# A two-layer encoder kernel: other dense blocks in layer 0, and its gathers moved into layer 1's attention stage

## The chip, the cores and the metric

The kernel runs on one core of one Trainium2 chip. The metric is device time in microseconds (us) of one execution, median of three runs. The core has a matrix engine (PE, with its weight loads as PEld), a vector engine (DVE), an activation engine (ACT), GpSimd (POOL) and SyncE (SP); 16 DMA engines move data between device memory and the on-chip memories.

## The reference

512 tokens of width 1024 go through two layers. Each layer has an attention part and an expert part, both with layer normalizations and a conditioning vector around them:

```python
h = _modulate(x, sh1, sc1)
mix = _hybrid_mixer(h, ...)            # MLA | short convolution | stick-breaking, then W_o
x = _layer_norm(DEEPNORM_ALPHA * x + (1 + g1) * mix, ...)
h = _modulate(x, sh2, sc2)
ffn = _peer(h, wq, k1, k2, u_tab, v_tab)
x = _layer_norm(DEEPNORM_ALPHA * x + (1 + g2) * ffn, ...)
```

The attention is causal in blocks of 128 tokens: block b needs the keys of blocks 0 to b. The expert part (PEER) gives every token 8 heads of 16 experts out of 16384: a query, scores against two sets of 128 keys, the top 16 of each, the top 16 of their sums. With the chosen experts' rows u and v (1024 numbers each),

```python
act = gelu(einsum('tkd,td->tk', u[experts], h))
out = einsum('tk,tkd->td', g * act, v[experts])
```

so a token's result sums 128 rows of v.

## The kernel before

**Blocks.** The tokens are four blocks of 128 (0 to 3). In the expert part two blocks of a layer are done *densely* and two by *gathers*; before, the dense ones are 1 and 2 in both layers (`DENSE`, L35).

**Dense blocks** (`dense`). For 256 tokens at once, all 16384 experts are worked through in 128 tiles of 128 experts. A tile's u and v rows (512 KB each) are loaded by SP; u is transposed on PE and split in two parts (ACT L819, DVE L821); three matmuls per slice make the scores (L831 to L833); ACT makes the Gelu, DVE multiplies by G, the gate weights spread out to a matrix over experts; two pairs of matmuls add the products with v (L849). G is made by `build` in three chunks: 32 builds ahead of the loop, 64 more beside the first 85 tiles. At the end each dense block's sum goes through `finish` (residual, layer normalization).

**Gathered blocks** (`experts`). For each of the 128 (head, rank) slots of a block, POOL issues an indirect DMA that fetches one row of u for each of 128 tokens (L696, 512 KB), and DVE multiplies it with h2 and sums (L698); then the same slot's row of v is fetched (L708) and added to the block's sum (L713). The slots go in four groups of 32: 32 u rows, a Gelu, 32 v rows. So a block is 256 gathers and a layer 512. Four buffers `g` (pool `gath`, L62) are shared by all; the block's sum `acc`, `h2`, `dots` and `wts` are single. The last slot is followed by `finish`, which writes the block's new x.

**Pacing** (`pace`). The gathers of a layer are one sequence, block by block. `EARLY[l]` of them are put ahead of the dense part and so run in the layer's own attention stage, as soon as the first gathered block's experts are known. 32 are paired with the 32 first builds, `LATE[l]` are left over for the next layer's attention stage (L956, L903), and the rest is spread evenly over the 128 tiles (L952). Within the paced part the DVE operation of a gather is ordered behind that of its tile. Before: 80 early, 350 in the loop and 50 late in layer 0; 110 early, 370 and 0 in layer 1.

**Attention stage.** Blocks 0 and 1 are normalized (`prepare`) and projected together, then attended one after the other; each goes through W_o (`output`), the normalizations (`between`), the queries (`queries`) and the top 16 (`topk`). Blocks 2 and 3 are prepared after block 1's attention and projected together: in `gemm` each weight tile serves block 2 and then block 3. `behind` puts that projection's first matmul behind the last query matmul of block 0. The top 16 of block 3 waits until the first builds are through (L950). In layer 0 the stage also computes the conditioning of both layers (`ada_side`) on DVE, ACT and POOL.

**Order.** The instruction order of each engine is planned at build time: a scheduler goes through the program with estimated times, and where several are ready takes the one that comes earlier in the program; on the chip each engine keeps that order. The late gathers stand ahead of the next layer's attention in the program.

Of the kernel before, what the change touches and what calls it, by code (L numbers as in the profile page):

```python
# [21 lines left out]
P = 128  # L22
# [3 lines left out]
NB = S // P  # L26
# [5 lines left out]
TG = 8  # L32
TI = 4
CUTS = (0, 43, 85, 128)
DENSE = (1, 2)  # L35
EARLY = (80, 110)
LATE = (50, 0)
WK = 4
ADK = 2
HB = 2  # L40
# [13 lines left out]
def body(ctx, tc, x, c, positions, ada_w, ada_b, w_in, q_norm_g, kv_norm_g, w_uq, w_ukv, conv_w,  # L54
         w_o, ln1_g, ln1_b, peer_wq, peer_k1, peer_k2, peer_u, peer_v, ln2_g, ln2_b, out):
    nc = tc.nc
# [89 lines left out]
    h2tok = [dram.tile([2, P, D], F32, name=f"h2tok{l}") for l in range(L)]  # L146
# [74 lines left out]
    def row_op(y, dst, src, i, op, mk=None, scalar=None, op0=None):  # L221
        for g in range(2):
            sl = slice(g * 512, (g + 1) * 512)
            pm = mk() if mk else A.ps.tile([P, 512], F32, name="prow", tag="mm", bufs=2)
            for c0 in range(2):
                r = 4 * i + 2 * g + c0
                nc.tensor.matmul(pm[:, c0 * 256:(c0 + 1) * 256], lhsT=sel[0:96, r:r + 1].to_broadcast([96, P]),
                                 rhs=y.rows[0:96, :], start=True, stop=True)
            if scalar is None:
                last = nc.vector.tensor_tensor(dst[:, sl], src[:, sl], pm, op=op)  # L230
            else:
                last = nc.vector.scalar_tensor_tensor(dst[:, sl], src[:, sl], scalar, pm, op0=op0, op1=op)
        return last
# [21 lines left out]
    def affine(y, dst, tmp, src, ig, ib, mk=None, pool=None):  # L255
        mean, r = moments(src, pool)
        row_op(y, tmp, src, ig, OP.mult, mk, mean, OP.subtract)
        return row_op(y, dst, tmp, ib, OP.add, mk, r, OP.mult)
# [89 lines left out]
    def exp_ln(first):  # L348
        ld = nc.scalar.preload_act_table_set("natural_log_exp_and_others")
        order(ld, first)  # L350
        return ld
# [222 lines left out]
    def between(y, b, rt, mk=None):  # L574
        l = y.l
        row_op(y, rt, rt, 7, OP.mult, mk)
        nc.vector.scalar_tensor_tensor(rt, xs[b], ALPHA, rt, op0=OP.mult, op1=OP.add)
        affine(y, xs[b], rt, rt, 0, 1, mk)
        h2 = A.work.tile([P, D], F32, name="h2d", tag="tok", bufs=2)
        affine(y, h2, h2, xs[b], 2, 3, mk)  # L580
        h2T = A.work.tile([P, KT, P], F32, name="h2T", tag="tok", bufs=2)
        transpose_cols(h2T, h2, KT, tag="tr" if mk else "mm")
        if b in DENSE:
            slot = DENSE.index(b) * P
            nc.sync.dma_start(h2scr[l][:, :, slot:slot + P], h2T)
        else:
            nc.sync.dma_start(h2tok[l][b // 2], h2)
        v1 = topp.tile([P, 2 * PH, TOPK], F32, name="tk_v", bufs=2)
        fi = topp.tile([P, PH, 2, TOPK], F32, name="tk_f", bufs=2)
        return h2T, v1, fi  # L590
# [89 lines left out]
    def experts(y, b, eidx, gw):  # L680
        def after(inst):
            if gate[0] is not None:
                tc.add_manual_dep(inst.ins, gate[0].ins.name,
                                  mybir.DependencyInfo(mybir.DependencyClass.NoSync, mybir.DependencyReason.DATA),
                                  reason="expert sums in pace with the dense tiles")

        h2 = pw.tile([P, D], F32, name="h2")
        nc.sync.dma_start(h2, h2tok[y.l][b // 2])
        acc = pw.tile([P, D], F32, name="acc")
        dots = pw.tile([P, PH, TOPK], F32, name="dots", bufs=1)  # L690
        wts = pw.tile([P, PH, TOPK], F32, name="wts", bufs=1)
        for h0 in range(0, PH, HB):
            slots = [(h, k) for h in range(h0, h0 + HB) for k in range(TOPK)]
            for j, (h, k) in enumerate(slots):
                g = gath.tile([P, D], F32, name="g")
                nc.gpsimd.indirect_dma_start(out=g, out_offset=None, in_=u_flat,  # L696
                                             in_offset=bass.IndirectOffsetOnAxis(ap=eidx[:, h, k:k + 1], axis=0))
                after(nc.vector.scalar_tensor_tensor(out=g, in0=g, scalar=1.0, in1=h2, op0=OP.mult, op1=OP.mult,  # L698
                                                     accum_out=dots[:, h, k:k + 1]))
                yield  # L700
            hs = slice(h0, h0 + HB)
            ge = nc.scalar.activation(wts[:, hs, :], dots[:, hs, :], AF.Gelu)
            if b == 0 and h0 < 2:
                exp_ln(ge)
            nc.vector.tensor_tensor(wts[:, hs, :], wts[:, hs, :], gw[:, hs, :], op=OP.mult)
            for j, (h, k) in enumerate(slots):
                g = gath.tile([P, D], F32, name="g")
                nc.gpsimd.indirect_dma_start(out=g, out_offset=None, in_=v_flat,  # L708
                                             in_offset=bass.IndirectOffsetOnAxis(ap=eidx[:, h, k:k + 1], axis=0))
                if h == 0 and k == 0:  # L710
                    r = nc.vector.tensor_scalar(acc, g, wts[:, h, k:k + 1], None, op0=OP.mult)
                else:
                    r = nc.vector.scalar_tensor_tensor(out=acc, in0=g, scalar=wts[:, h, k:k + 1], in1=acc,  # L713
                                                       op0=OP.mult, op1=OP.add)
                after(r)
                if h < PH - 1 or k < TOPK - 1:
                    yield
        tc.cur_priority -= 1000000
        finish(y, b, acc, lambda: psx.tile([P, 512], F32, name="prow", tag="ex"), pw)
        tc.cur_priority += 1000000  # L720
        yield

    def finish(y, b, acc, mk, pool):
        row_op(y, acc, acc, 4, OP.mult, mk)
        nc.vector.scalar_tensor_tensor(acc, xs[b], ALPHA, acc, op0=OP.mult, op1=OP.add)
        r = affine(y, xs[b], acc, acc, 5, 6, mk, pool)
        if y.l == L - 1:
            nc.sync.dma_start(out[0, b * P:(b + 1) * P, :], xs[b])
        return r
# [164 lines left out]
    def pace(ex, mark, n):  # L894
        gate[0] = mark
        for _ in range(n):
            next(ex)

    ada_first(range(4))
    for l in range(L):  # L900
        if l:
            open_attention(l)
            late()  # L903
        y = layer_setup(l)

        def pick(b, v1, fi):
            return topk(l, v1, fi, b, b not in DENSE)

        res = [None] * NB
        for b in (0, 1):  # L910
            prepare(y, b)
        layer_keys(y)
        ps = project(y, (0, 1))
        if l + 1 < L:
            ada_side(0, range(4, 12))
        layer_rows(y)
        behind = None
        for p in ps:
            b = p[0]
            attend(y, *p)  # L920
            if b == 1:
                for b2 in (2, 3):
                    prepare(y, b2)
            h = between(y, b, output(y, b, p[2]))
            r = queries(y, *h, range(4))
            if b == 0:
                behind = r
            res[b] = pick(b, *h[1:])
        p2, p3 = project(y, (2, 3), behind)
        if l + 1 < L:  # L930
            ada_side(1, range(12))
        attend(y, *p2)
        h = between(y, 2, output(y, 2, p2[2]))
        queries(y, *h, range(2))
        attend(y, *p3)
        rt = output(y, 3, p3[2])
        queries(y, *h, range(2, 4))
        res[2] = pick(2, *h[1:])
        h = between(y, 3, rt, lambda: A.ps.tile([P, 512], F32, name="prow", tag="at", bufs=2))
        queries(y, *h, range(4))  # L940
        res[3] = partial(pick, 3, *h[1:])
        A.stack.close()
        dn = dense(y, DENSE, res)
        ex = chain.from_iterable(experts(y, b, *res[b]) for b in range(NB) if b not in DENSE)
        pace(ex, None, EARLY[l])
        groups = 2 * P // TG
        for _ in range(groups):
            mark = next(dn)
            pace(ex, mark, 1)
        with tc.issue_after(mark.ins):  # L950
            res[3] = res[3]()
        n = 2 * 2 * NSLOT - EARLY[l] - LATE[l] - groups  # L952
        for a, mark in enumerate(dn):
            if a < NK:
                pace(ex, mark, (a + 1) * n // NK - a * n // NK)
        late = partial(pace, ex, mark, LATE[l])  # L956
        if not l + 1 < L:
            late()
# [22 lines left out]
```

## Time and profile before

| | |
|---|---|
| median of 3 runs | 3552.92 us (3548.99 to 3555.07) |
| profiled execution | 3562.45 us, its span 3560.7 us |
| granted clock of PE, mean | 0.921 of full speed |
| PE / DVE / POOL / ACT busy | 88% / 77% / 41% / 26% of the span |
| moved by DMA | 1012 MB, mean 284 GB/s |
| layer 0: attention stage, first build | 0 to 687.2 us |
| layer 0: dense loop's combining matmuls | 783.0 to 1782.9 us |
| layer 1: attention stage, first build | to 2442.7 us |
| layer 1: dense loop's combining matmuls | 2540.3 to 3536.0 us |

The span is the time from the first to the last instruction of the profiled execution. A busy share is an average over stages with different limits, so the table is read by stage. A group's row names the line, the engine, the operation, output and inputs, the count, the busy time and mean duration, and then the engine's idle time just before it with what ended most of it.

### The profile page before, as it was taken

How to read it: one execution, taken by the hardware profiler on the slowest of the kernel's cores; microseconds unless marked ns; L12 is line 12 of the kernel's file. 1: busy time of each engine (PE TensorE's matmuls, PEld its weight loads, DVE VectorE, ACT ScalarE, POOL GpSimd, SP SyncE). 2: the span in 40 equal slices, each digit the busy share in tenths (PEclk: the TensorE clock that was granted, in tenths of full speed). 3: DMA queues.
4: the chain of work that ended last, by engine and by line, in shares of the span. 5: the costliest groups of instructions: out<-in, count | busy, mean ns of one | idle time of the engine just before them, and what ended most of it. 6: DMA issues, size and time to landing. Idle time of an engine off the chain costs nothing.

```text
span 3560.7 us, 54292 instructions
## 1 busy us (share of the span) xinstructions
PE 3131.7 (88%) x19708; PEld 2331.2 (65%) x19708; DVE 2753.5 (77%) x6085; ACT 925.9 (26%) x1860; POOL 1455.3 (41%) x1347
## 2 busy tenths in 40 slices
PE   6889778659999999999948896786799999999998
PEld 3567546547777777777736784565577777777775
DVE  4668996999777867676775589889998787776777
ACT  2342432222222222222122223312222222222221
POOL 1025573255434334444451045533454444444443
PEclk9989879859999999999969996897799999999998
DMA  8778978568888888899985586885789988889997
GB/s 269 221 231 261 312 253 278 178 196 293 314 314 312 307 285 313 314 344 347 337 286 194 177 297 208 288 297 172 256 284 335 333 320 310 319 309 336 360 351 257
DMA packets 430171, 1012.13 MB, mean 284 GB/s; under 512 B 40504, under 2 KB 229192, under 8 KB 429904
## 3 DMA queue, kind: packets, MB, share of 16 engines
q0 software_dynamic: 147456, 536.94, 42.3%
q1 hardware_dynamic: 282448, 471.73, 39.3%
q8 instruction: 156, 2.56, 0.3%
q14 instruction: 111, 0.91, 0.1%
HBM read 1002.06 MB, written 6.34 MB: 283 GB/s over the span
## 4 chain that ended last, share of the span: by engine, by line
PE 18%; DVE 11%; DMA 9%; issue 8%; POOL 3%; ACT 1%; SPq 0%; POOLq 0%; DVEq 0%; ACTq 0%
PE pm L157 5%; DMA g<-in_peer_v,eidx 5%; PE acc L849 5%; DVE acc L713 2%; POOL g L696 2%; DVE g L698 2%; DMA g<-in_peer_u,eidx 2%; DMA wt<-in_peer_wq 1%; PE sp L831 1%; PE sp L832 1%; PE sp L833 1%; PE utp L817 1%; DMA wt<-in_w_in 1%; DVE o L797 1%; DVE tk_ef L668 1%
## 5 line engine op out<-in xcount | busy, mean ns | idle before, releaser
L708 POOL DMA_INDIRECT g<-in_peer_v,eidx x512 | 616.0, 1203 | 806.0 <-DVE acc L713 553.3
L849 PE MATMUL acc<-v,ge 128*128 128x512 f32 x2048 | 926.7, 595 | 0.9 <-DMA v<-in_peer_v 0.5
L696 POOL DMA_INDIRECT g<-in_peer_u,eidx x512 | 582.2, 1137 | 765.6 <-DVE g L698 546.7
L713 DVE SCALAR_TENSOR_TENSOR acc<-g,wts,acc 128x1024 f32<-128x1024 f32 x508 | 673.7, 1326 | 149.6 <-DMA g<-in_peer_v,eidx 146.1
L698 DVE SCALAR_TENSOR_TENSOR g<-g,h 128x1024 f32<-128x1024 f32 x512 | 622.2, 1227 | 152.6 <-DMA g<-in_peer_u,eidx 151.3
L831 PE MATMUL sp<-hh,uh 128*128 128x256 f32 x2048 | 612.9, 299 | 4.2 <-ACT ge L835 4.2
L849 PEld LDWEIGHTS acc<-v,ge 128*128 128x128 f32 x2048 | 371.5, 191 | 367.3 <-issue 366.5
L833 PE MATMUL sp<-hh,ul 128*128 128x256 f32 x2048 | 594.8, 290 | 0.0
L832 PE MATMUL sp<-hl,uh 128*128 128x256 f32 x2048 | 583.4, 285 | 0.0
L819 ACT CAST uh<-utp 128x512 fp32r<-128x512 f32 x512 | 304.7, 596 | 866.5 <-PE utp L817 728.9
L821 DVE TENSOR_TENSOR ul<-utp,uh 128x512 fp32r<-128x512 f32 x512 | 346.4, 683 | 117.0 <-ACT uh L819 116.3
L831 PEld LDWEIGHTS sp<-hh,uh 128*128 128x128 f32 x2048 | 391.3, 191 | 10.2 <-ACT ge L835 5.1
L832 PEld LDWEIGHTS sp<-hl,uh 128*128 128x128 f32 x2048 | 391.5, 191 | 4.8 <-issue 4.8
L833 PEld LDWEIGHTS sp<-hh,ul 128*128 128x128 f32 x2048 | 390.7, 191 | 0.0
L817 PE MATMUL utp<-ident,u 128*128 128x128 f32 x2048 | 304.9, 278 | 25.1 <-DVE ul L821 21.9
L804 PEld LDWEIGHTS <-o 128*128 128x128 bf16 x4608 | 222.0, 117 | 152.2 <-DVE o L797 79.0
L806 ACT COPY G<-pg 128x344 f32<-128x344 f32 (+1 forms) x192 | 147.1, 766 | 618.0 <-PE pg L804 618.0
L804 PE MATMUL pg<-o,o 128*128 128x43 bf16 (+1 forms) x4608 | 235.8, 219 | 80.4 <-DVE o L797 75.7
L817 PEld LDWEIGHTS utp<-ident,u 128*128 128x128 f32 x2048 | 239.4, 143 | 96.4 <-issue 62.9
L157 PE MATMUL pm<-wt,hT 128*128 128x256 f32 (+1 forms) x1024 | 234.6, 383 | 21.9 <-DMA wt<-in_w_in 14.8
L157 PE MATMUL pm<-wt,h2T 128*128 128x256 f32 x1024 | 238.6, 389 | 14.6 <-DMA wt<-in_peer_wq 14.5
L157 PEld LDWEIGHTS pm<-wt,h2T 128*128 128x128 f32 x1024 | 195.8, 195 | 48.5 <-DMA wt<-in_peer_wq 16.3
(235 smaller groups left out, 3451.8 us busy)
## 6 DMA issues: line engine op xcount, KB each, us to landing
u<-in_peer_u SPq DMA_DIRECT2D x256, 512.0 KB
v<-in_peer_v SPq DMA_DIRECT2D x256, 512.0 KB
wt<-in_peer_wq SPq DMA_DIRECT2D x128, 512.0 KB
adw<-in_ada_w SPq DMA_DIRECT2D x160, 256.0 KB
wt<-in_w_o SPq DMA_DIRECT2D x64, 512.0 KB
wt<-in_w_in SPq DMA_DIRECT2D x56, 512.0 KB
wt<-in_ada_w SPq DMA_DIRECT2D x16, 512.0 KB
g<-in_peer_u,eidx POOLq DMA_INDIRECT x512, 6.9
```

The lines of the kernel that those rows point to most:

```text
L157: r = nc.tensor.matmul(pm[:, c0:c0 + m], lhsT=lhsT[:, k0 + k, :], rhs=wt[:, k, :m], start=k0 + k == 0, stop=k0 + k == KT - 1)
L696: nc.gpsimd.indirect_dma_start(out=g, out_offset=None, in_=u_flat, in_offset=bass.IndirectOffsetOnAxis(ap=eidx[:, h, k:k + 1], axis=0))
L698: after(nc.vector.scalar_tensor_tensor(out=g, in0=g, scalar=1.0, in1=h2, op0=OP.mult, op1=OP.mult, accum_out=dots[:, h, k:k + 1]))
L708: nc.gpsimd.indirect_dma_start(out=g, out_offset=None, in_=v_flat, in_offset=bass.IndirectOffsetOnAxis(ap=eidx[:, h, k:k + 1], axis=0))
L713: r = nc.vector.scalar_tensor_tensor(out=acc, in0=g, scalar=wts[:, h, k:k + 1], in1=acc, op0=OP.mult, op1=OP.add)
L804: nc.tensor.matmul(pg[:, tt, 0:n], lhsT=o2[:, tt // TI, :, tt % TI], rhs=o1a[:, tt // TI, p, 0:n, tt % TI], start=tt == 0 and p == 0, stop ...
L817: nc.tensor.transpose(pt[:, j * P:(j + 1) * P], u[:, k * P:(k + 1) * P], ident)
L821: nc.vector.tensor_tensor(ul.rearrange("p j t -> p (j t)"), pt, uh.rearrange("p j t -> p (j t)").bitcast(F32), op=OP.subtract)
L831: nc.tensor.matmul(sp, lhsT=uh[:, j, :], rhs=hh[:, k, :], start=k == 0, stop=False)
L832: nc.tensor.matmul(sp, lhsT=uh[:, j, :], rhs=hl[:, k, :], start=False, stop=False)
L833: nc.tensor.matmul(sp, lhsT=ul[:, j, :], rhs=hh[:, k, :], start=False, stop=k == KT - 1)
L849: nc.tensor.matmul(acc[i][g], lhsT=w[:, i * P:(i + 1) * P], rhs=v[:, g * 512:(g + 1) * 512], start=a == 0, stop=a == NK - 1)
```

## The change

Layer 0's dense blocks become 0 and 1, its gathered blocks 2 and 3; layer 1 keeps 1 and 2 dense, 0 and 3 gathered. Since block 2's experts are known only at the end of layer 0's attention stage, none of layer 0's gathers is put there (`EARLY[0]` 80 to 0). `LATE[0]` goes from 50 to 120, and the dense loop of layer 0 gets 512 - 0 - 120 - 32 = 360 instead of 350. The other edits look up which blocks are which by layer.

```diff
-DENSE = (1, 2)
-EARLY = (80, 110)
-LATE = (50, 0)
+DENSE = ((0, 1), (1, 2))
+GATHERED = tuple(tuple(b for b in range(4) if b not in d) for d in DENSE)
+EARLY = (0, 110)
+LATE = (120, 0)
...
-        if b in DENSE:
-            slot = DENSE.index(b) * P
+        if b in DENSE[l]:
+            slot = DENSE[l].index(b) * P
             nc.sync.dma_start(h2scr[l][:, :, slot:slot + P], h2T)
         else:
-            nc.sync.dma_start(h2tok[l][b // 2], h2)
+            nc.sync.dma_start(h2tok[l][GATHERED[l].index(b)], h2)
...
-        nc.sync.dma_start(h2, h2tok[y.l][b // 2])
+        nc.sync.dma_start(h2, h2tok[y.l][GATHERED[y.l].index(b)])
...
-            if b == 0 and h0 < 2:
+            if b < 2 and h0 < 2:
                 exp_ln(ge)
...
-            return topk(l, v1, fi, b, b not in DENSE)
+            return topk(l, v1, fi, b, b in GATHERED[l])
...
-        dn = dense(y, DENSE, res)
-        ex = chain.from_iterable(experts(y, b, *res[b]) for b in range(NB) if b not in DENSE)
+        dn = dense(y, DENSE[l], res)
+        ex = chain.from_iterable(experts(y, b, *res[b]) for b in GATHERED[l])
         pace(ex, None, EARLY[l])
```

## Rows read from the trace of the kernel before

**Rows 1.** The page: busy time of each engine over the span, its share, instructions.

```profile
PE 3131.7 (88%) x19708; PEld 2331.2 (65%) x19708; DVE 2753.5 (77%) x6085; ACT 925.9 (26%) x1860; POOL 1455.3 (41%) x1347
```

**Rows 2.** Busy time by stretch (us from the start), granted clock, DMA share, GB/s.

```profile
330.00:600.00 270.00, 215.53 (x927) 147.37 (x927) 230.92 (x622) 96.40 (x204) 161.08 (x146) 0.85 0.89 295
1784.00:1832.00 48.00, 6.62 (x24) 3.45 (x23) 40.43 (x67) 8.51 (x12) 33.73 (x36) 0.52 0.80 254
1832.00:1925.00 93.00, 78.81 (x359) 62.50 (x360) 54.16 (x100) 25.46 (x68) 32.91 (x30) 0.92 0.86 292
1925.00:2022.00 97.00, 83.31 (x448) 65.62 (x447) 47.05 (x156) 34.37 (x88) 6.96 (x16) 0.92 0.41 131
2022.00:2151.00 129.00, 122.44 (x617) 102.86 (x615) 100.53 (x400) 32.09 (x77) 46.17 (x50) 0.99 0.84 283
2151.00:2240.00 89.00, 58.98 (x172) 34.23 (x173) 86.67 (x188) 25.27 (x53) 51.55 (x49) 0.58 0.64 196
```

**Rows 3.** L849's matmuls in the two dense loops, PE busy, PEld busy, same columns.

```profile
783.00:1733.00 950.00, 434.27 (x960) 174.24 (x960) 0.99 0.88 316
2540.00:3486.00 946.00, 435.14 (x961) 174.30 (x962) 1.00 0.90 326
```

**Rows 4.** DVE groups in 330:600: busy, mean ns, idle before and its releaser.

```profile
L698 DVE SCALAR_TENSOR_TENSOR g<-g,h 128x1024 f32<-128x1024 f32 x48 | 60.6, 1268 | 13.2 <-DMA g<-in_peer_u,eidx 13.1
L713 DVE SCALAR_TENSOR_TENSOR acc<-g,wts,acc 128x1024 f32<-128x1024 f32 x31 | 46.7, 1507 | 1.3 <-DMA g<-in_peer_v,eidx 1.2
```

**Rows 5.** The chain that ended last, shares by line, in 2151:2240.

```profile
by line: issue 19.6%; DVE acc L713 17.0%; DVE tk_ef L668 12.5%; PE z L551 9.2%; DMA g<-in_peer_u,eidx 5.9%; DVE g L698 5.2%; DVE tk_hot L665 5.0%; PE sc L504 3.5%; DVE mx L506 3.3%; DVE tk_ti L619 3.2%; DVE sp L546 2.3%; PE po L561 2.0%; DV
```

**Rows 6.** DVE time of the second gathers' sums (L713) in two stretches.

```profile
1776.00:1922.00 146.00, 41.01 (x32) 0.80 0.85 284
2076.00:2378.00 302.00, 69.89 (x45) 0.84 0.86 291
```

**Rows 7.** DVE time of the first gathers' products (L698), two instructions each.

```profile
1776.00:1922.00 146.00, 25.55 (x42) 0.80 0.85 284
2076.00:2378.00 302.00, 78.12 (x128) 0.84 0.86 291
```

**Rows 8.** DVE's timeline around block 3's last sums in layer 1.

```profile
1852.70 1.28 DVE L713 SCALAR_TENSOR_TENSOR acc<-g,wts,acc 128x1024 f32<-128x1024 f32 x1
...
1869.95 1.28 DVE L713 SCALAR_TENSOR_TENSOR acc<-g,wts,acc 128x1024 f32<-128x1024 f32 x1 [2.13 <-DMA g<-in_peer_v,eidx]
...
1919.87 1.28 DVE L713 SCALAR_TENSOR_TENSOR acc<-g,wts,acc 128x1024 f32<-128x1024 f32 x1 [1.94 <-DMA g<-in_peer_v,eidx]
```

**Rows 9.** The page: gathers issued by POOL, count, median us to landing.

```profile
g<-in_peer_u,eidx POOLq DMA_INDIRECT x512, 6.9
```

**Rows 10.** DVE's timeline: block 3's end, and the normalizing of blocks 2, 3.

```profile
1934.16 0.75 DVE L232 SCALAR_TENSOR_TENSOR xs<-acc,rs_r,prow 128x512 f32<-128x512 f32 x1 [0.62 <-PE prow L227]
...
1975.53 1.28 DVE L244 BATCH_NORM_STATS2 bnst<-xs 128x6 f32<-128x512 f32 x2
```

**Rows 11.** PE's timeline: projections of two blocks begin (hT); layer 1's first build.

```profile
1832.14 3.75 PE L157 MATMUL pm<-wt,hT 128*128 128x256 f32 x8 [4.16 <-DMA wt<-in_w_in]
...
2021.54 2.75 PE L157 MATMUL pm<-wt,hT 128*128 128x256 f32 x12
...
2442.68 1.26 PE L804 MATMUL pg<-o,o 128*128 128x43 bf16 x24
```

**Rows 12.** ACT's timeline: first exponentials of blocks 0 and 2; last column of hT.

```profile
1928.11 0.36 ACT L510 ACTIVATE pr<-sc,mx 128x128 f32<-128x128 f32 x1
...
1983.89 2.96 ACT L274 ACTIVATE hT<-pt,sh,sc 128x128 f32<-128x128 f32 x8
...
2151.63 0.58 ACT L510 ACTIVATE pr<-sc,mx 128x384 f32<-128x384 f32 x1 [1.69 <-DVE mx L506]
```

**Rows 13.** DVE groups in 2151:2240 that belong to block 1's top 16.

```profile
L668 DVE TENSOR_REDUCE tk_ef<-tk_pick 128x8 f32<-128x400 f32 x16 | 13.8, 863 | 0.0
...
L665 DVE TENSOR_TENSOR tk_hot<-iotaj,tk_tib 128x400 bf16<-128x400 bf16 x16 | 5.6, 350 | 0.0
```

## The prediction, made before the changed kernel ran

> **What bounds the kernel now.** I read first the page's busy times: PE is busy 88% of the span, DVE 77%, POOL 41% [rows 1]. These are averages over four unlike parts (two attention stages, two dense stages), so the next view is that of the stretches, and then the rows inside each.
>
> The dense loops are PE's. In layer 0's, 960 of the combining matmuls take 950 us; in layer 1's, 961 take 946 us, at a granted clock of 0.99 and 1.00 [rows 3]. The code paces 350 gathers beside the first and 370 beside the second. Twenty gathers more cost no time: PE sets the pace and the gathers ride along.
>
> The attention stages have no such master. Where layer 0's 80 early gathers run (330 to 600 us) DVE is busy 231 of 270 us and PE 216 at a clock of 0.85. Where layer 1's attention runs with no gather (1925 to 2022) DVE is busy 47 of 97 us and PE 83, at 0.92, with the DMA engines used 0.41 [rows 2]. The reader should see two things there: gathers fill DVE, and a stretch without them runs PE denser and at a better clock.
>
> Gathers themselves go through four buffers. A gather lands a median 6.9 us after POOL issues it [rows 9], its sum then takes 1.28 us [rows 8]: 8.2 us for a buffer, so four of them let one gather by every 2.05 us, before any waiting for a turn on POOL or DVE. In fact 53 gathers took 146 us at the start of layer 1 and 110 took 302 us later there, 2.75 us each in both [rows 6, 7]. The fastest run is nine turns from 1852.70 to 1869.95, 1.92 us each, while DVE had nothing else to do [rows 8].
>
> **The change, part by part.** It moves 80 gathers (48 products and 32 sums, each one indirect DMA of 512 KB on POOL and one wide operation on DVE) out of layer 0's attention stage; 10 go into layer 0's dense loop, 70 into layer 1's attention stage, ahead of the 110 that are there.
>
> *Layer 0's attention stage.* The moved work is 60.6 + 46.7 us of DVE with 14.5 us of waiting for landings in front [rows 4], about 122 us of the 270. That isn't all on the path. From below: PE's 215.5 us at the density of the gather-free stretch (83.3 of 97, 0.86) would fill 251 us, a gain of 19; at that stretch's clock too, 215.5 x 0.85 / 0.92 / 0.86 = 232 us, a gain of 38. From above: layer 1 from 2151 to 2240 holds 32 gathers, and 17.0 + 5.9 + 5.2 = 28% of the chain there is theirs, 25 of 89 us, 0.78 us each [rows 5]; for 80 that is 62 us. (The chain's "issue" share, 19.6%, may hold more of them; with all of it the bound is 106 us.) I take 46, between 38 and 62 and nearer the PE value, since PE is what remains. The Gelu of the first group and its table changes go with it; I put them at nothing beside that.
>
> *Layer 0's dense loop.* 10 more gathers: nothing, by the pair of loops above [rows 3]. PE hides them. If that cover were gone each would cost its DVE turn of 1.3 us, 13 us in all.
>
> *Layer 1's attention stage.* Here a data dependence counts. Block 3 of layer 0 is gathered last, so its x is final only when the last late gather is summed; then come its finish, the normalizing of blocks 2 and 3, and the input projection of both (a weight tile is used for block 2 and then block 3, so PE goes nowhere with one). Before, the 50 late gathers end at 1921.15 [rows 8], x at 1934.91 [rows 10], the normalizing is done by 1986.85 [rows 10, 12] and the projection begins at 2021.54, behind block 0's queries [rows 11]: slack, so that those 50 cost little. Now 70 more follow 1921.15. At 2.3 us each (half way between the fast 1.92 and the usual 2.75, because DVE is half free in that stretch but not empty) that is 161 us: 2082. Then 13.8 us for the finish (1921.15 to 1934.91) and 11.3 us for the normalizing (1975.53 to 1986.85) [rows 8, 10, 12]: 2107, 86 us later than before. The ends: at 1.92 us 2080, at 2.75 us 2139.
>
> What does it cost? Before, PE did block 1's queries in between, and from the projection's start to block 2's first exponential it took 130 us (2021.54 to 2151.63). The like projection of blocks 0 and 1, alone, took 96 us (1832.14 to 1928.11) [rows 11, 12]. While PE waits for x it can do block 1's output and queries, so I use 96: 2203 instead of 2152, +51 us. Behind it something comes back: block 1's top 16 (13.8 + 5.6 us of DVE [rows 13], in a stretch where DVE is busy 87 of 89 us [rows 2]) is then done during the wait. I take 15 of these 19 as returned; the ends are 0 and 19. So +36 for the stage. The 110 early gathers, which start behind the late ones at about 2085 instead of 2076, still end by 2390, before the builds (2442.68 before [rows 11]), and cost nothing new. Queued behind the moved gathers: on POOL the small steps of the normalizations and block 0's top 16, on DVE all of attention 0 and 1, who pass the delay to PE; but PE would have to wait for block 3 anyhow, which covers them. SP has one load of h2 for each gathered block as before.
>
> Sum: -46 + 0 + 36 = -10 us. The profiled execution took 3562.45 us, its span 3560.7, the median of the runs 3552.92; from the profiled one that gives 3552, from the median 3543.
>
> One thing bears against the sum. After the stretch from 1784 to 1832, where PE was busy 6.6 of 48 us and the clock was granted at 0.52 (near the lower level, 1.2 of 2.4 GHz), the next 93 us had 0.92 [rows 2]: 0.08 x 93, about 7 us lost to the clock. A new PE wait for block 3 could cost those 7 us once more, which makes the sum -3. The Trainium skill, "TensorE: Matmul & The Clock Gate", section "HAM oscillation — how this bites in real kernels", says that waits between bursts of matmuls put the array back to the lower rate, so that each burst begins slow; by that rule this case would be the rule and not the exception, and the trace agrees so far as the 0.52 and 0.92 go. I leave it out of the sum because PE has block 1's output and queries to do in the wait, and keep it as a rival.
>
> **The rivals.** *Block 3 holds everything (slower).* If the projection of blocks 2 and 3 stands ahead of block 1's queries in PE's fixed order, as it stood among them before (2021 to 2151), PE waits with the queries behind it, and the 130 us count: 2107 + 130 = 2237, +86, with nothing returned. Net -46 + 86 = +40, 3593 from the median. For it: PE and DVE keep a written order, and 70 gathers end some 86 us past the slack. Against it: queries come earlier in the program. It decides from a net delay of 46 us at block 2's attention. *The wait is mostly hidden:* gathers at the fast turn, 1.92 us: 2080 + 96 = 2176, +25, less 15, and -46: -36, 3517. For it, DMA at 0.41 and DVE half idle in 1925 to 2022; against it, 2.75 in both long series. *Layer 0 gains little:* PE density alone, 19 us; -19 + 36 = +17, 3570. For it, PE is already busy 80% there; against it, DVE's 86%. *The clock:* PE idles before block 3's projection and gets the lower clock, -3, 3550; for it, the 0.52 above, against it, the work that PE has meanwhile.
>
> **How the numbers follow.** My forecast, a small gain, has 0.40; block 3 holding everything 0.28; the hidden wait 0.15; little gain in layer 0 0.10; the clock 0.07. The time is the forecast's, 3543. Its own range, with the ends of its unknown costs, is 3518 to 3563. As cases of both signs are near, the range for 8 in 10 reaches to 3500 (hidden wait, with more than 46 in layer 0) and to 3598 (block 3, a little beyond 3593). A measurement of this kernel tells about 0.2%, 7 us, from no change. Faster: 0.29 of the forecast's 0.40, 0.15 of the hidden wait, 0.02 of the clock: 0.46. Same: 0.08, 0.05 of the clock, 0.04 of the others: 0.17. Slower: the rest, 0.37.
>
> **What would show it.** Layer 0's first build should come at about 641 instead of 687 us, with DVE well below 0.86 before it. Layer 0's dense loop should keep about 950 us for 960 combining matmuls. In layer 1 the last late sum should fall about 300 us after the dense loop's end, PE should be idle before the projection of blocks 2 and 3, and the stage from dense loop to first build should be some 36 us longer than before. The prediction is wrong if that stage grows by 80 or more, if layer 0's shrinks by under 25, or if the dense loop stretches.

## The result and the profile after

The changed kernel takes 3619.76 us (median of 4 runs, 3613.65 to 3624.91), the kernel before 3553.24 in the same comparison: a ratio of 1.0177, interval 1.0155 to 1.0200. It is slower by 1.8%, 66 us, where 10 us of gain were forecast, and 22 us above the end of the range.

Where the time went is read by stages of the two profiled executions (spans 3560.7 and 3619.8 us). A stage is cut at the first build of the dense blocks' tables and at ACT's last copy of the dense sums; the rows for the cuts stand below. Line numbers are those of each kernel: L805 here is L804 of the kernel before.

| us | before | after | difference |
|---|---|---|---|
| layer 0, attention, to the first build | 687.2 | 655.9 | -31.3 |
| layer 0, dense | 1096.8 | 1092.9 | -3.9 |
| layer 1, attention, to block 2's first exponential | 367.6 | 470.1 | +102.5 |
| layer 1, attention, from there to the first build | 291.1 | 276.5 | -14.6 |
| layer 1, dense, and the tail | 1118.1 | 1124.4 | +6.3 |

The sum is +59.0, the difference of the spans. One stage lost it: layer 1's attention, +88 us where the forecast had +36.

The page's busy times of the kernel after, against [rows 1]:

```profile
PE 3126.6 (86%) x19708; PEld 2324.0 (64%) x19708; DVE 2750.9 (76%) x6085; ACT 933.2 (26%) x1865; POOL 1419.4 (39%) x1347
```

PE, DVE and POOL have no more work than before (3131.7, 2753.5 and 1455.3 us then), so 59 us of span are waits that were not there. The stretches of the kernel after, with the columns of [rows 2], show where. Layer 0's dense loop is first, then layer 1's attention in order of time:

```profile
749.00:1749.00 1000.00, 987.01 (x6580) 730.01 (x6581) 776.02 (x1286) 236.72 (x452) 438.17 (x378) 0.99 0.89 321
1749.00:1797.00 48.00, 7.24 (x26) 4.01 (x26) 39.90 (x68) 8.39 (x11) 33.87 (x36) 0.52 0.80 250
1797.00:1890.00 93.00, 78.35 (x356) 62.30 (x355) 52.55 (x103) 25.19 (x68) 38.26 (x35) 0.90 0.91 310
1890.00:1987.00 97.00, 63.77 (x309) 46.19 (x309) 72.89 (x119) 29.96 (x75) 50.91 (x52) 0.76 0.82 274
1987.00:2047.00 60.00, 50.55 (x232) 40.83 (x231) 50.44 (x215) 7.48 (x16) 21.76 (x20) 0.95 1.02 360
2047.00:2098.00 51.00, 7.33 (x29) 3.87 (x28) 48.18 (x94) 2.72 (x5) 28.52 (x31) 0.54 0.34 107
2098.00:2219.00 121.00, 105.46 (x500) 85.04 (x498) 94.26 (x355) 33.16 (x78) 49.59 (x49) 0.94 0.92 320
```

The first 141 us (1749 to 1890) are those of [rows 2] again, 1784 to 1925. The next 97 differ: before, PE did 83.3 us of work there beside 47.1 of DVE's; now 63.8 beside 72.9. Then comes a hole: from 2047 to 2098 PE works 7.33 of 51 us. The timeline of PE, ACT and DVE after shows the cuts, the hole, and what filled it:

```profile
655.87 0.69 PE L805 MATMUL pg<-o,o 128*128 128x43 bf16 x12
...
1747.74 1.07 ACT L886 COPY fa<-acc 128x512 f32<-128x512 f32 x2 [0.27 <-PE acc L850]
...
2020.74 4.43 PE L158 MATMUL pm<-wt,hT 128*128 128x256 f32 x22
...
2027.70 5.35 PE L158 MATMUL pm<-wt,cat 128*128 128x256 f32 x24
...
2051.81 1.22 DVE L578 SCALAR_TENSOR_TENSOR rt<-xs,rt 128x1024 f32<-128x1024 f32 x1
...
2070.82 1.40 DVE L714 SCALAR_TENSOR_TENSOR acc<-g,wts,acc 128x1024 f32<-128x1024 f32 x1
...
2073.92 0.59 PE L228 MATMUL prow<-rows,sel 96*128 96x256 bf16 x2 [24.43 <-DVE acc L231]
...
2088.33 1.26 DVE L245 BATCH_NORM_STATS2 bnst<-rt 128x6 f32<-128x512 f32 x2
2089.52 0.73 DVE L233 SCALAR_TENSOR_TENSOR xs<-acc,rs_r,prow 128x512 f32<-128x512 f32 x1
...
2098.07 2.51 PE L158 MATMUL pm<-wt,hT 128*128 128x256 f32 x8
...
2119.41 1.89 PE L158 MATMUL pm<-wt,h2T 128*128 128x256 f32 x8
...
2218.91 0.58 ACT L511 ACTIVATE pr<-sc,mx 128x384 f32<-128x384 f32 x1 [0.60 <-DVE mx L507]
...
2495.41 1.26 PE L805 MATMUL pg<-o,o 128*128 128x43 bf16 x24
```

Read it from the top. The input projection of blocks 2 and 3 (hT) starts at 2020.74 and does its first 32 matmuls; block 1's output (cat) follows. Then PE comes to a small matmul of block 3's finish (L228, the row that spreads a scale) and stands 24.43 us for it, because block 3's last sum ends at 2072.2. The projection goes on at 2098.07, and block 1's queries (h2T) come only at 2119.41. They need nothing of block 3, but their input was not there earlier either: block 1's output is summed with its x (rt, L578) at 2053.03, and DVE starts the next step of its normalization (bnst<-rt) at 2088.33, behind steps of block 3's finish in its own fixed order. Before, the same two steps stood next to each other, 1963.55 and 1965.30. So block 1 was held on DVE as well as on PE. PE's waits in 2047:2098 of the kernel after (total us, times, longest):

```profile
PE prow L228 <- DVE acc L231: 25.5, 2, 24.4
PE prow L228 <- DVE acc L233: 8.1, 2, 6.2
PE prow L228 <- DVE xs L233: 4.3, 2, 2.9
```

These three are 37.9 of the 51 us, all at L228.

### The profile page after: what moved, and what is told of

The parts are those of the page before. It is cut to its first block, busy times and chain, and to the rows that moved or that the text cites. A ratio compares the mean times of both kernels' runs of the same rounds, so it can differ in the third digit from the quotient of the medians.

```text
span 3619.8 us, 54318 instructions
## 1 busy us (share of the span) xinstructions
PE 3126.6 (86%) x19708; PEld 2324.0 (64%) x19708; DVE 2750.9 (76%) x6085; ACT 933.2 (26%) x1865; POOL 1419.4 (39%) x1347
## 4 chain that ended last, share of the span: by engine, by line
PE 15%; DVE 13%; DMA 10%; issue 10%; POOL 3%; ACT 1%; SPq 0%; POOLq 0%; DVEq 0%; ACTq 0%
DMA g<-in_peer_v,eidx 5%; PE pm L158 4%; PE acc L850 4%; DVE acc L714 3%; DMA g<-in_peer_u,eidx 3%; POOL g L697 2%; DVE g L699 2%; DVE tk_ef L669 1%; PE sp L832 1%; PE sp L834 1%; PE sp L833 1%; PE utp L818 1%; DMA wt<-in_w_in 1%; DMA wt<-in_w_o 1%; DMA wt<-in_peer_wq 1%
## 5 line engine op out<-in xcount | busy, mean ns | idle before, releaser
L850 PE MATMUL acc<-v,ge 128*128 128x512 f32 x2048 | 927.0, 595 | 4.6 <-DVE ge L838 3.4
L709 POOL DMA_INDIRECT g<-in_peer_v,eidx x512 | 586.9, 1146 | 833.6 <-DVE acc L714 509.3
L850 PEld LDWEIGHTS acc<-v,ge 128*128 128x128 f32 x2048 | 371.8, 191 | 372.9 <-issue 369.2
L805 PEld LDWEIGHTS <-o 128*128 128x128 bf16 x4608 | 221.5, 117 | 147.2 <-DVE o L798 77.8
L805 PE MATMUL pg<-o,o 128*128 128x43 bf16 (+1 forms) x4608 | 235.2, 219 | 75.0 <-DVE o L798 72.9
L158 PEld LDWEIGHTS pm<-wt,hT 128*128 128x128 f32 x1024 | 190.4, 196 | 53.1 <-DMA wt<-in_w_in 16.2
```

The lines of the kernel that those rows point to most:

```text
L158: r = nc.tensor.matmul(pm[:, c0:c0 + m], lhsT=lhsT[:, k0 + k, :], rhs=wt[:, k, :m], start=k0 + k == 0, stop=k0 + k == KT - 1)
L805: nc.tensor.matmul(pg[:, tt, 0:n], lhsT=o2[:, tt // TI, :, tt % TI], rhs=o1a[:, tt // TI, p, 0:n, tt % TI], start=tt == 0 and p == 0, stop ...
L850: nc.tensor.matmul(acc[i][g], lhsT=w[:, i * P:(i + 1) * P], rhs=v[:, g * 512:(g + 1) * 512], start=a == 0, stop=a == NK - 1)
```

## The experiments

Each kernel's stages are cut like those above; "layer 1" is layer 1's attention stage, 658.7 us before and 746.6 after. "Block 3" is the time from the end of layer 0's dense stage to block 3's final x, 150.9 and 341.4 us. Kernels without an interval ran once, and are read by their stages alone. The planner makes the order of the instructions anew for each kernel, so a difference between two of them is that of the edit together with the order that it led to.

**How many gathers are really late.** The first two take the changed kernel and give the moved gathers to the dense loop:

```diff
-LATE = (120, 0)
+LATE = (50, 0)      # and (85, 0) in the second
```

> The changed kernel with 50 late gathers instead of 120, so 430 in layer 0's dense loop. Theory A (block 3 of layer 0 is summed too late and holds the projection of blocks 2 and 3): layer 1's attention stage falls back from 747 us to about 659, its length before, and layer 0's attention stage keeps its gain of 31 us. If the dense loop hides 70 more gathers, the time is about 3553 - 31 = 3522; if the loop is then set by the gathers (430 at 2.35 us each are 1010 us, the loop has 1000), it is longer by 10 to 60 us and the time 3530 to 3580. Theory B (70 gathers cost DVE time wherever they run beside other work): the 88 us come back in the dense loop in part, since DVE has 776 of 1000 us busy there, and the time stays at 3590 or more.

> The changed kernel with 85 late gathers, 395 in the dense loop. Theory A: a late gather costs nothing up to about 78 and then its turn, some 2.7 us; layer 1's attention stage is 659 + 7 x 2.7 = about 678 us (up to 690), the time about 3540. Theory B (DVE time of each): the cost grows evenly with the number, 35 of the 70 gathers cost 44 of the 88 us, stage about 703, time about 3565.

Measured: 3573.19 us, ratio 1.0043 (1.0025 to 1.0061), and 3571.86, ratio 1.0040 (1.0018 to 1.0061). Layer 1 took 711.3 and 718.2, block 3 298.5 and 298.0. The loop was asked to take 430 and 395 gathers; in both it took 378, was no longer for it (the dense stage 1089.0 and 1088.0 against 1092.9), and left 102 gathers to run late. In the two traces PE, DVE, ACT and POOL each run the same instructions in the same order: the planner, by its estimated times, put 378 gathers beside the loop and the rest behind it, whatever was asked. So both kernels are the same experiment, 102 late gathers, and the slope that they were to give could not be read from them. They show that the loop takes 378 gathers without becoming longer; that the chip would not take more there is not shown. And they show how far two executions of one order differ: 7 us in layer 1's attention stage.

The next keeps the dense blocks of before and moves only the gathers:

```diff
 DENSE = (1, 2)
-EARLY = (80, 110)
-LATE = (50, 0)
+EARLY = (10, 110)
+LATE = (120, 0)
```

> The kernel before with its own dense blocks 1 and 2, but 10 early and 120 late gathers in layer 0 instead of 80 and 50: the move of 70 gathers alone, without the new choice of blocks. Theory A: block 3 is the late one here too, so layer 1's attention stage takes about 747 us as in the changed kernel; layer 0's attention stage loses 70 of its 80 gathers and is shorter by about 27 of the 31 us; the time is about 3553 - 27 + 88 = 3614. A rival (the other choice of dense blocks costs it, since layer 1's blocks 0 and 1 both come out of the dense part): the stage is clearly under 747, by 20 us or more.

Measured: 3605.38 us; layer 0's attention 649.2, layer 1 744.1, block 3 337.5, as the first theory expected. The late gathers alone cost layer 1 its 85 us; the choice of dense blocks adds no more than two executions of one order differ.

Two more keep the kernel before and move fewer of its early gathers, into the loop alone: 28, as many as the 378 allow, and 50:

```diff
-EARLY = (80, 110)
+EARLY = (52, 110)   # and (30, 110)
```

> The kernel before, its own blocks, with 52 early gathers in layer 0 instead of 80, 50 late as before, so 378 in the dense loop instead of 350. The changed kernel with 50 late gathers showed that the loop takes 378 without becoming longer. If 28 early gathers cost what 80 cost in layer 0 (31 to 38 us, 0.4 to 0.5 each), the kernel is faster by 11 to 14 us, 0.3 to 0.4%: 3539 to 3542 against 3553. If the loop falls behind with the changed order of blocks, some end up late and the gain is under 5 us.

> The kernel before, its own blocks, with 30 early gathers in layer 0 and 50 late, so 400 in the dense loop. The loop has taken 378 to 385 in about 1000 us, 2.6 us each. If that is its limit, some 10 to 20 of the 400 end up late, block 3 is final 30 to 50 us later than before, and what the attention stage of layer 0 gains (another 9 us over 52 early) is given back: 3538 to 3550. If the loop can take 400, the time is about 3532.

Measured: with 52, 3541.32 us (12 runs), ratio 0.9964 (0.9947 to 0.9981); with 30, 3543.54 (10 runs), ratio 0.9966 (0.9948 to 0.9985). Both beat both kernels. Both times lie where they were expected. Together with the runs above they are a table of late gathers against layer 1:

| kernel | asked of the loop | really late | block 3 | layer 1 |
|---|---|---|---|---|
| before | 350 | 50 | 150.9 | 658.7 |
| 52 early | 378 | 53 | 160.2 | 662.2 |
| 30 early | 400 | 68 | 193.8 | 673.7 |
| after with 50, 85 | 430, 395 | 102 | 298.5, 298.0 | 711.3, 718.2 |
| old blocks, 120 | 350 | 120 | 337.5 | 744.1 |
| after | 360 | 120 | 341.4 | 746.6 |

The first 18 gathers past 50 cost (673.7 - 658.7) / 18 = 0.8 us each, the last 18 about (746.6 - 714.8) / 18 = 1.8 (714.8 is the mean of the two kernels with 102). The first 18 cost nothing by a wait for block 3: with 68 late, the projection of blocks 2 and 3 begins at 252.1 us, 34 us behind block 3's last column of hT (218.4), and before it began at 237.6, 35 us behind it (202.9). They delay blocks 0 and 1. Past about that point block 3 is waited for, and most of a gather's turn is on the path.

**What a late gather costs: the dependence.** This one is the changed kernel, with block 3's expert result of layer 0 left out of its x (the gathers and sums still run, and nothing waits for them there):

```diff
-        r = affine(y, xs[b], acc, acc, 5, 6, mk, pool)
+        r = affine(y, acc if (y.l, b) == (0, 3) else xs[b], acc, acc, 5, 6, mk, pool)
```

> The changed kernel, with block 3's expert result of layer 0 left out of x: the finish of that block is computed in full but written to its own sum and not to x, so layer 1 goes on with block 3 as it was after layer 0's attention. All 120 late gathers still run. Theory A (the data dependence holds the projection): the projection of blocks 2 and 3 begins right behind block 0's queries, about 2021 us, with no PE wait of 50 us before it, and layer 1's attention stage falls from 747 us to 660 to 690. Theory B (DVE is filled by the 70 extra sums, dependence or not): the projection may begin earlier, but the stage stays above 725.

Measured: 3570.91 us, layer 1 701.7, between the two theories. The timeline of PE in this kernel at the projection, and at the first build:

```profile
2019.71 5.35 PE L158 MATMUL pm<-wt,h2T 128*128 128x256 f32 x24
2024.90 4.91 PE L158 MATMUL pm<-wt,hT 128*128 128x256 f32 x22
...
2452.68 1.24 PE L805 MATMUL pg<-o,o 128*128 128x43 bf16 x24
```

The hole is gone: the projection starts 274 us after the dense stage's end and runs on. 45 of the 88 us come back with the dependence; 43 stay. Part of these is visible here: the projection stands directly behind block 0's queries (h2T), which end 274 us after the dense stage; before, the projection stood at 238 [rows 11].

**The sums on DVE and the bytes.** The late gathers' products and sums were cut to 64 of their 1024 columns, first with block 3 free as in the last kernel, then alone (the dependence kept):

```diff
+                w_ = slice(0, few[0])      # few[0]: 64 while the late gathers run, else D
-                after(nc.vector.scalar_tensor_tensor(out=g, in0=g, scalar=1.0, in1=h2, ...
+                after(nc.vector.scalar_tensor_tensor(out=g[:, w_], in0=g[:, w_], scalar=1.0, in1=h2[:, w_], ...
```

> The kernel with block 3 free (its expert result of layer 0 left out of x), and the DVE operations of the 120 late gathers cut to 64 of 1024 columns, so that most of their products and sums are left out; every gather is still issued and landed. Theory C (what is left without the dependence, 43 us of layer 1's attention stage, is DVE time of the extra sums): the stage falls from 702 us to 660 to 675, near its 659 of before. Theory D (it is the 37 MB of transfers beside the weights, or POOL's issues): it stays at 690 or more.

> The changed kernel with the same cut to 64 columns in the late gathers' DVE operations, but with the dependence on block 3 kept. Theories A and C together: the gathers run at the turn of their buffers, 2.1 to 2.3 us, so block 3 is final about 265 to 290 us after the dense loop instead of 341, and layer 1's attention stage takes 675 to 700 us instead of 747. Theory D: the rate stays near 2.7 us and the stage above 730.

Measured with block 3 free: 3549.98 us, layer 1 688.5, nearly what the second theory expected, and block 0's queries end at 239. So the 34 to 36 us of delay on block 0's path are the sums' time on DVE, but the stage gets only 13 us of them. Measured with the dependence: 3627.55 us, layer 1 751.7, block 3 337.5, as without the cut, though block 0's queries end at 234. While block 3 is waited for, DVE's time is worth nothing. PE's longest wait in this kernel:

```profile
2061.85 0.59 PE L228 MATMUL prow<-rows,sel 96*128 96x256 bf16 x2 [41.71 <-DVE acc L231]
```

PE got earlier to the same matmul and stood there 41.7 us instead of 24.4. The time that DVE spends on a late gather is not what sets its turn. The next two also let each late gather fetch 64 columns, 256 bytes a token in place of 4 KB, first with block 3 free, then alone:

```diff
-                nc.gpsimd.indirect_dma_start(out=g, out_offset=None, in_=u_flat,
+                nc.gpsimd.indirect_dma_start(out=g[:, 0:few[0]], out_offset=None, in_=table[few[0]][0],
```

> Block 3 free and the late DVE operations cut to 64 columns, as before, and now each of the 120 late gathers also fetches 256 bytes a token instead of 4 KB (other rows than the right ones): POOL's issues stay, the transfers nearly go. Theory D (the 30 us that layer 1's attention stage keeps over its 659 of before are transfers beside the weights): the stage falls from 688 to 655 to 668 us. Theory E (they come from POOL's issues and the order of the instructions): it stays at 680 or more.

> The changed kernel with the dependence on block 3 kept, late gathers cut in DVE columns and in bytes as above. If the turn of a buffer is mostly the landing of 512 KB, the 120 late gathers now take some 1.3 to 1.7 us each, block 3 is final about 190 to 220 us after the dense loop instead of 341, before the projection of blocks 2 and 3 asks for it, and layer 1's attention stage takes 660 to 685 us instead of 747 although the dependence is there. If landing is a fixed latency that bytes hardly change, the rate stays near 2.4 us, block 3 is final after 300 us and the stage is above 710.

Measured: 3556.39 us, layer 1 684.3 with block 3 free; 3550.14, layer 1 683.4, block 3 219.6 with the dependence. The first 200 us of layer 1, in the kernel with narrow sums and whole rows and then in the one with narrow sums and short rows (columns of [rows 2]):

```profile
1749.00:1949.00 200.00, 142.42 (x704) 108.83 (x702) 77.45 (x268) 60.82 (x153) 87.87 (x104) 0.85 0.89 305
```

```profile
1749.00:1949.00 200.00, 121.75 (x528) 92.94 (x528) 68.67 (x289) 50.39 (x120) 121.02 (x135) 0.77 0.40 106
```

DVE has nearly the same little work in both; the DMA engines go from 0.89 to 0.40. POOL issues 78 gathers there with whole rows (2.6 us each) and 116 with short ones (about 1.7). The timeline of block 3's end, the projection and the first build in the kernel with short rows:

```profile
1966.00 0.73 DVE L233 SCALAR_TENSOR_TENSOR xs<-acc,rs_r,prow 128x512 f32<-128x512 f32 x1
...
2015.86 4.48 PE L158 MATMUL pm<-wt,hT 128*128 128x256 f32 x20
...
2430.60 1.26 PE L809 MATMUL pg<-o,o 128*128 128x43 bf16 x24
```

Block 3 is now ready 49 us before PE gets to the projection, and with that the dependence costs nothing: freed or kept, the stage takes the same 684 us, with the same order on PE and POOL. So 68 us (751.7 to 683.4), of the 93 that the kernel with narrow sums had over 658.7, hang on how fast the late gathers land. The bytes beside the weights are worth little by themselves: with block 3 free, short rows took the stage from 688.5 only to 684.3.

What stays is 25 us over 658.7, with no wait for block 3, no wide sums and few bytes. It can't be read as a rest of the changed kernel's loss, since the two kernels with short rows bring a delay of their own. Block 0's first exponential, with whole rows and then with short ones, both with narrow sums and the dependence kept:

```profile
1879.71 0.37 ACT L511 ACTIVATE pr<-sc,mx 128x128 f32<-128x128 f32 x1
```

```profile
1909.14 0.37 ACT L511 ACTIVATE pr<-sc,mx 128x128 f32<-128x128 f32 x1
```

These are 127.3 and 162.0 us behind the dense stage (144.1 before), and block 0's queries end at 234 and 269. POOL, which also does small steps of the normalizations, is busy 121 of the first 200 us with short rows and 88 with whole ones; whether that is the reason, or the other order that the planner made, no run here says.

**The order around the hole.** Two kernels put the late gathers behind block 1's attention in the program, in the changed kernel and in the fast one with 52 early:

```diff
-            late()                 # at the layer's start
...
             if b == 1:
+                if l:
+                    late()
                 for b2 in (2, 3):
                     prepare(y, b2)
```

> The changed kernel (120 late gathers, dependence kept) with the late gathers put into the program behind block 1's attention of layer 1, just ahead of the preparing of blocks 2 and 3, instead of ahead of the whole layer; so the planner gives blocks 0 and 1 the engines first, and block 1's normalizations and queries no longer stand behind the finish of block 3 on PE and DVE. Theory F (25 of the 88 us are work of block 1 that is queued behind block 3's finish and so can't fill the wait): block 1's queries run during the wait, from block 3's projection to block 2's first exponential it takes about 96 us instead of 121, and layer 1's attention stage is 715 to 730 us instead of 747; time about 3595. Rival G (the late gathers lose their turns to the attention and end later by as much): block 3 is final 370 us or more after the dense loop, and the stage is 745 or longer.

> The kernel before with 52 early gathers (which was 0.36% faster than before) and the same new place of the 50 late ones in the program. Theory F: blocks 0 and 1 of layer 1 get on earlier, block 3 still in time, layer 1's attention stage 645 to 660 us instead of 662, time 3527 to 3541. Rival G: the late gathers take longer and hold the projection of blocks 2 and 3: stage 670 or more.

Measured: 3623.40 us, ratio 1.0189 (1.0152 to 1.0226), layer 1 748.1; and 3545.82, ratio 0.9970 (0.9952 to 0.9989), layer 1 665.1. The order on the engines hardly changed (block 3 336.6 and 161.9; in the second kernel PE and POOL keep their order to the last instruction), so the move in the program did not make the test that it was meant to make, and decides nothing. The last kernel writes the order out: in layer 1, the late gathers and the preparation of blocks 2 and 3 are written behind block 1's queries, and block 3's finish comes on PE behind the first half of them:

```diff
+                if hold[0] is not None and y.l < L - 1 and A.layer:
+                    order(mm_, hold[0])     # mm_: the finish's matmul; hold[0]: block 1's queries, first half
...
+        if l:                               # behind block 1's queries, not at the layer's start
+            late()
+            for b2 in (2, 3):
+                prepare(y, b2)
```

> The changed kernel (120 late gathers, dependence kept), with block 3's finish tied behind the first half of block 1's queries in PE's order (the first matmul of the finish is ordered behind them), and the preparing of blocks 2 and 3 behind it in the program. Theory F (block 1's normalizations and queries stand behind the finish of block 3 on PE and so can't fill the wait): block 1's queries begin before block 3 is final, some 310 to 330 us after the dense loop, from block 3's normalized columns to block 2's first exponential it takes 96 to 110 us instead of 119, and layer 1's attention stage is 720 to 740 us instead of 747 (block 3 itself may be final up to 15 us later). If the time behind block 3's columns stays at 119 or more although the queries went first, the order on PE is not what made it long.

Measured: 3604.51 us, layer 1 739.0. DVE's and PE's timelines in this kernel, block 1's normalization and queries, then the finish and the projection:

```profile
2047.07 1.27 DVE L251 BATCH_NORM_STATS2 bnst<-rt 128x6 f32<-128x512 f32 x2
...
2079.57 7.07 PE L161 MATMUL pm<-wt,h2T 128*128 128x256 f32 x32
...
2105.18 0.38 PE L231 MATMUL prow<-rows,sel 96*128 96x256 bf16 x2 [3.05 <-DVE acc L237]
...
2139.45 2.56 PE L161 MATMUL pm<-wt,hT 128*128 128x256 f32 x8
```

Block 1's normalization now goes on at once (2047.07 instead of 2088.33) and its queries run inside the wait; from the last column of block 3's hT to block 2's first exponential it takes 90 us instead of 119 (393.4 to 483.2 against 351.5 to 470.1). But the finish waits for the queries in its turn, and block 3 is 40 us later (381.8 against 341.4), where at most 15 were expected. So block 2's first exponential comes 13 us later (483.2 against 470.1). The stage is 8 us shorter only because 21 come back behind it (255.7 us from there to the first build, against 276.5); 8 is hardly more than the 7 by which two executions of one order differed.

## Why the prediction was wrong

The cause that decided was in the prediction: block 3's x is final only when the last late gather is summed, and the projection needs it. Freeing that one dependence gives 45 us back; landing the gathers sooner, with narrow sums, 68. The forecast's case was wrong, and its first rival, that block 3 holds everything, is near what happened: layer 1 +88 us for its +86. That the two numbers are so close is partly luck: block 3's last column came 28 us later than put there, the stretch from it to block 2's exponential took 118.6 us and not 130, and 14.6 us came back behind it where the rival had nothing. What was wrong with the steps:

- **The turn of a late gather, 2.3 us.** The last late sum ended 137.2 us after the dense stage before (1921.15 of [rows 8], 1784.0) and 323.4 after (2072.2, 1748.8): 186 us for 70 gathers, 2.66 each, where 161 were put. That is +25 us, and block 3's finish, 18.0 us to its last x instead of 13.8, adds 4. The 2.3 was put half way between 1.92 and 2.75 because DVE is half free in that stretch. The 1.92 was itself a miscount: from 1852.70 to 1869.95 nine sums start, which is eight turns, 2.16 us each; half way would have been 2.45, 172 us for the 70. With almost all of DVE's work on these gathers gone, the turn stayed at 2.6; with a sixteenth of the bytes as well, and another order by the planner, it fell to 1.7. So the landing sets a good part of it, and DVE's free time was no reason to leave the 2.75 of [rows 6, 7].
- **"PE can do block 1's output and queries" in the wait.** It did the output. The queries came after the wait: block 1's normalization, which they need, stood behind block 3's finish in DVE's fixed order (rt ready at 2053.03, gone on with at 2088.33), and on PE too the finish's matmuls stood ahead of them. So the projection's going on to block 2's exponential took 120.8 us (2098.07 to 2218.91) and not 96: +25. With block 1's normalization and queries ahead of the finish, that stretch is 29 us shorter, so it is shown that the order made it long. That run turned the order on both engines at once, so which of the two held the queries is not told apart; and in the one order that was tried, block 3's finish then waits for the queries and the gain is lost again.
- **Layer 0's gain, 46 us.** It was 31; nine further kernels with the same layer 0 up to there gave 28.6 to 36.1. The measured 31 lies between PE's density alone, 19, and PE's density at the better clock, 38; the 62 from the chain's share was too high, and the 46 leaned on it. That is 15 us of error.
- **The cover for blocks 0 and 1.** That the moved sums delay attention 0 and 1 was said, and that PE's wait for block 3 covers it. Both hold: block 0's queries end at 272 us instead of 238, and taking that delay away changes nothing while block 3 is waited for (751.7 against 746.6). With the wait gone, it is 13 us.
- **What held.** The dense loops kept their pace to 1% with ten gathers more in layer 0, as L850's matmuls show against [rows 3] in stretches of the same length:

```profile
749.00:1699.00 950.00, 435.28 (x963) 175.06 (x964) 0.99 0.89 321
2590.00:3536.00 946.00, 431.59 (x952) 172.63 (x952) 0.99 0.90 323
```

  The normalizing took 10.1 us from x to the last column of hT where 11.3 were put. The give-back behind block 2's exponential, put at 15, was 14.6.
- **The clock.** After the hole, in which the granted clock fell to 0.54 (near 1.2 of 2.4 GHz), the next 121 us had 0.94: 0.06 x 121 = 7 us, the price that the clock rival gave. The Trainium skill, "TensorE: Matmul & The Clock Gate", section "HAM oscillation — how this bites in real kernels", says that waits put the array back to the lower rate and the next burst begins slow; the trace agrees so far as these two rows go. No run took the clock apart from the wait, so these 7 us are argued, and they lie inside the 120.8.

With the measured terms the sum is -31.3 - 3.9 + 102.5 - 14.6 + 6.3 = +59: the forecast's -10, and then 15 for layer 0, 25 and 4 for block 3's last gather and finish, 25 for the queries. The other terms nearly cancel. The 6 us of layer 1's dense stage and tail lie in no term of the prediction, but the fifteen profiled kernels have 1112 to 1124 us there with the same work, so they are no more than spread. Still open: what layer 1 loses without the dependence. With block 3 free and narrow sums it keeps 30 us, 12 of them ahead of block 2's first exponential and 18 behind it; with short rows as well 25, all of them ahead of it (397 to 399 us instead of 368).

## What to carry to other kernels

Transfers beside a loop that another engine paces can be free: here the loop took up to 382 gathers where 350 were used and was no longer for them. How many go there is decided by the planner and not by the number in the program, so the number that really went has to be read from the trace. Moving 28 gathers into it, of which 25 went there, gained 0.36%, while moving 70 past the loop's end lost 1.8%. Work that is moved behind a boundary has to be followed to the last thing that needs it, and in a fixed order one has to ask not only what an engine could do in the new wait, but what stands behind the waiting instruction, on every engine that the work passes through: block 1's queries, which needed nothing of block 3, came 66 us after their block's output was summed, because steps of block 3's finish stood ahead of theirs on DVE and PE. A turn that one series shows under the same load (2.75 us, twice) was a better price here than a value between it and the fastest run.

## What the runs showed of the hardware

A gather of 512 KB (4 KB for each of 128 tokens) through four buffers took 2.7 us a turn with whole sums on DVE and 2.6 with sums of 64 columns, with the DMA engines busy 0.87 and 0.89 of the time (first 200 us of layer 1). With 256 bytes a token it still took about 1.7 us a turn, at a DMA share of 0.40: a sixteenth of the bytes buys a third of the turn. Layer 0's dense loop, where PE is busy 987 of 1000 us, had 375 to 382 gathers beside it in the four kernels that asked for more than 360, and was no longer for them than with 350. These numbers are the planner's; whether the chip would take more was not tried.
